# Holding the second layer's modulation sums on VectorE behind the feed-forward norm's inverse roots

## The chip, the core and the metric

The kernel runs on one core of a Trainium2 chip. The core has a matrix engine (TensorE, PE in the rows), two elementwise engines (VectorE, DVE; ScalarE, ACT), GpSimd (POOL) and SyncE (SP), which issues the transfers from HBM. Each engine takes its instructions in the order in which they stand in its own list, and starts one when the semaphores it waits for are there. The metric is the device time of one execution in microseconds (us).

## The reference

Two layers of a diffusion backbone over 256 latent and 256 context tokens of width 1024. What matters here is the conditioning of each layer and the feed-forward part of the first:

```python
def _rmsnorm(x, g):
    y = xf * lax.rsqrt(jnp.mean(xf * xf, axis=-1, keepdims=True) + EPS)
    return (y * g.astype(jnp.float32)).astype(x.dtype)
...
def _modulate(x, g, shift, scale):
    return _rmsnorm(x, g) * (1 + scale) + shift
...
def _adaln(cond, w_mod, b_mod):
    return jnp.split(jax.nn.silu(cond) @ w_mod + b_mod, N_MOD, axis=-1)
...
def _swiglu(x, w1, w3, w2):
    return (jax.nn.silu(x @ w1) * (x @ w3)) @ w2
...
# first layer, after its mixer
h = h + gt1 * o_lat
u_lat = _modulate(h, norm_ffn_g[layer], sh2, sc2)
g = g + cgt1 * o_ctx
tokens = jnp.concatenate([_modulate(g, norm_ffn_g[layer], csh2, csc2), u_lat], axis=1)
y = _swiglu(tokens, ffn_w1[j], ffn_w3[j], ffn_w2[j])
```

The second layer has its own `_adaln`: a product of a conditioning vector with a 1024 x 6144 matrix. It depends on nothing that the first layer computes.

## The kernel before, in words

The feature dimension lies on the 128 partitions, the 512 tokens along the free dimension: columns 0 to 255 are the context tokens (stream 0), 256 to 511 the latent ones (stream 1). `H` holds the residual, `Uhi` and `Ulo` the normed and modulated tokens, split in two parts, so that each matrix product is three matmuls (L162, L163, L164). The weights are loaded as `raw`, cast to `whi` on ScalarE and split off as `wlo` on VectorE (both L141); `whi` and `wlo` have six buffers each, `raw` four, which the modulation matrix shares. A scheduler at build time sets the order of every engine's list from the order of the code and from priorities; the order on the chip is then fixed.

The feed-forward norm of the first layer is `norm_T`, for stream 0 and then stream 1: squares on ScalarE (L318, L321), their sums on VectorE (L322, L324, tile `sqa`), a sum over the partitions on TensorE (L289, `ps_hg`), the inverse root on VectorE, and its spreading over the partitions on TensorE (L295), then per block of 128 features a product on VectorE (L336, `u`), the shift on ScalarE (L337, `Uhi`) and the remainder on VectorE (L338, `Ulo`). The inverse root (`rsqrt`, tile `rsq`) is eleven small VectorE operations, each on the result of the one before, L302, L303 and three rounds of

```python
        dve.tensor_tensor(b, y, y, op=OP.mult)
        dve.scalar_tensor_tensor(b, b, -0.5, v, op0=OP.mult, op1=OP.mult)
        latest_y[:] = [dve.scalar_tensor_tensor(y, b, 1.5, y, op0=OP.add, op1=OP.mult)]
```

which are L305, L306 and L307. Behind the norm stand the first four column tiles of the feed-forward layer (two of `w1`, two of `w3`). They are computed for stream 0 alone and then for stream 1 alone, 96 matmuls of 256 columns each; the tiles after them take all 512 columns at once. ScalarE takes the silu of the `w1` tiles (L756, `s`), VectorE multiplies it with the `w3` tiles (L759), and the result is split into `hh` (ScalarE) and `hl` (VectorE), both L167.

The second layer's modulation is worked out in the background by `mod1`, on VectorE: a block is 512 of the 6144 columns, and its sum over the 1024 rows is made of eight operations in each half, with two sums (`macc`, one for each conditioning vector) for blocks 0 to 3: L238 begins a sum, L240 adds to it (128 x 512). A half is 1 MB of `raw`, whose load is issued by SyncE (L113) in one list with the loads of the feed-forward weights (L116). When a block's sums are there, TensorE adds them over the partitions (L256) and the columns go to `modc` (L265). The generator is stepped between the tiles of the feed-forward layer. Block 0 lies in the last products of the mixer, block 1 in the feed-forward norm, blocks 2 to 7 in the feed-forward layer, 8 to 11 in the attention of the second layer. At the end stands the second layer's expert part, which streams its weights from HBM (`moe_u`, `moe_d`).

The prediction gives the line numbers of this kernel; those of the changed one are one or two higher from L237 on.

Of the kernel before, what the change touches and what calls it, by code (L numbers as in the profile page):

```python
# [15 lines left out]
OP = mybir.AluOpType  # L16
# [47 lines left out]
def body(tc, A, out):  # L64
    nc = tc.nc
    ctx = ExitStack()
    pe, act, dve, pool, sp = nc.tensor, nc.scalar, nc.vector, nc.gpsimd, nc.sync

    def sb(name, side="left"):
        return tc.tile_pool(name=name, bufs=1, side=side, reuse_waits="tile")  # L70
# [15 lines left out]
    def ps(tag, n=512):  # L86
        t = banks["pool"].tile([128, 512], F32, name="ps_" + tag, tag=tag, bufs=banks["bufs"][tag])
        return t[:, :n] if n != 512 else t
# [8 lines left out]
    def V(name, a=0, n=None):  # L97
        o, m = _VEC[name]
        return vec[:, o + a:o + a + (m if n is None else n)]
# [7 lines left out]
    def stream(src, kt=0, cols=0):  # L107

        turns.append(turns.pop(0))
        raw = turns[-1].tile([128, 2048], F32, name="raw", tag="raw", bufs=RING if len(turns) == 2 else None)  # L110
        if not kt:
            v = raw.rearrange("p (k c) -> p k c", k=4)
            sp.dma_start(v, src)  # L113
            return v
        v = raw[:, :kt * cols].rearrange("p (k c) -> p k c", k=kt)
        sp.dma_start(v, src.rearrange("(k p) c -> p k c", p=128))  # L116
        return v
# [28 lines left out]
    @contextmanager  # L146
    def behind(*ops):

        with ExitStack() as x:
            for op in ops or latest:  # L150
                x.enter_context(tc.issue_after(op.ins))
            yield
# [66 lines left out]
    def mod1(*groups):  # L219


        todo = [(g, blk, half) for g in groups for blk in g for half in range(2)]

        def load(i):
            g, blk, half = todo[i]
            return stream(A["w_mod"][1, blk, half])

        w, sums = load(0), []
        for i, (g, blk, half) in enumerate(todo):
            yield  # L230
            streams = range(2 if blk < 4 else 1)
            if half == 0:
                acc = [up.tile([128, 512], F32, name="macc", tag="macc", bufs=2) for _ in streams]
            for j in range(4):
                for s in streams:
                    c = csig[:, 4 * half + j, s:s + 1]
                    if half + j == 0:  # L237
                        dve.tensor_scalar(acc[s], w[:, j, :], c, None, op0=OP.mult)  # L238
                    else:
                        dve.scalar_tensor_tensor(acc[s], w[:, j, :], c, acc[s], op0=OP.mult, op1=OP.add)  # L240
            if i + 1 < len(todo):
                w = load(i + 1)
            if half == 0:
                continue
            sums += [(blk, s, a) for s, a in enumerate(acc)]
            if blk != g[-1]:
                continue
            p = ps("x")
            if blk in (4, 5, 8, 9, 10, 11):
                pe.matmul(p, ones1, acc[0], start=True, stop=True)  # L250
                r = {2: gt1r, 4: GF, 5: gt2r}[blk // 2][:, 512 * (blk % 2):512 * (blk % 2) + 512]
                dve.tensor_tensor(r, r, p, op=OP.add)
            else:
                n = 4 // len(sums)
                for q in range(4):
                    pe.matmul(p[32 * q:32 * q + 32, :], ones1[:, 0:32], sums[q // n][2], start=True, stop=True,  # L256
                              tile_position=(0, 32 * q))
                row = modp.tile([128, 512], F32, name="modrow", tag="modrow")
                act.copy(row, p)
                p = ps("x")  # L260
                for f in range(4):
                    pe.transpose(p[:, 128 * f:128 * f + 128], row[:, 128 * f:128 * f + 128], ident)
                v = p.rearrange("p (a g b) -> p g a b", a=4, g=4)
                for q, (b, st, _) in enumerate(sums):
                    dve.tensor_tensor(modc[1][:, 4 * b:4 * b + 4, st], v[:, n * q, :, 0], V("bm1", 4 * b, 4), op=OP.add)  # L265
            sums = []
# [40 lines left out]
            latest_y[:] = [dve.scalar_tensor_tensor(y, b, 1.5, y, op0=OP.add, op1=OP.mult)]  # L307
        return y

    latest_y = []  # L310

    def squares(tp, h, s, acc=None):

# [13 lines left out]
    def stream_rstd(tp, h, s):  # L327
        return rstd_rows(squares(tp, h, s), V("invd"), 2)

    def modulate(tp, h, rstd, s, ks, G, layer, which_shift, uhi, ulo, of=None):  # L330
        c = slice(256 * s, 256 * s + 256)
        of = of or c
        for k in ks:
            u = tp.tile([128, 2, NL], F32, name="u", tag="sq", bufs=3)[:, 0]
            shift = modc[layer][:, 8 * which_shift + k, 1 - s:2 - s]
            dve.scalar_tensor_tensor(u, h[:, k, of], G[:, k, 1 - s:2 - s], rstd, op0=OP.mult, op1=OP.mult)  # L336
            act.activation(uhi[:, k, c], u, AF.Identity, bias=shift)  # L337
            dve.scalar_tensor_tensor(ulo[:, k, c], u, shift, uhi[:, k, c].bitcast(F32), op0=OP.add, op1=OP.subtract)  # L338

    def norm_T(tp, *a):  # L340
        with tc.high_priority():
            for s in range(2):
                modulate(tp, a[0], stream_rstd(tp, a[0], s), s, range(KT), *a[1:])
# [7 lines left out]
    with sb("n0") as tp:  # L351
# [5 lines left out]
        acc = tp.tile([128, NTOK], F32, name="sqacc")  # L357
# [320 lines left out]
    acc = sop.tile([128, NTOK], F32, name="sqacc")  # L678
# [58 lines left out]

    finish()
    background.append(mod1((0,), (1,), (2,), (3,), (4,), (5,), (6, 7)))
    G2 = gain_cols("G2", 0, 4, "gf0")  # L740
    Uhi = up.tile([128, KT, NTOK], F32R, name="Uhi", tag="Uhi")
    Ulo = up.tile([128, KT, NTOK], F32R, name="Ulo", tag="Ulo")
    norm_T(nrm, H, G2, 0, 3, Uhi, Ulo)
    ffx = ExitStack()
    ffp = ffx.enter_context(sb("ffp", "right"))
    held = []
# [54 lines left out]
    Ulo = up.tile([128, KT, NTOK], F32R, name="Ulo", tag="Ulo")  # L801
    norm_T(nrm, H, G3, 1, 0, Uhi, Ulo)
    background.append(mod1((8,), (9,), (10,), (11,)))
    for _ in range(2):
        step()
# [94 lines left out]
    for g in range(2):  # L900
        c = slice(512 * g, 512 * g + 512)
# [109 lines left out]
    for g in range(2):  # L1011
# [3 lines left out]
        for t in range(2):  # L1015
# [7 lines left out]
            c = slice(512 * g, 512 * g + 512)  # L1023
# [315 lines left out]
    acc = [ps("mm") if i < 3 else ps("x") for i in range(4)]  # L1339
    for p, (t, g) in zip(acc, SETS):  # L1340
        scatter(p, DTS[1], t, g, 2, True, True)
    for p, (t, g) in zip(acc, SETS):
        c = slice(512 * g, 512 * g + 512)
# [144 lines left out]
```

## Time and profile before

| | |
|---|---|
| time, median of 3 runs | 1668.04 us (1666.72 to 1668.6) |
| the profiled execution | 1669.41 us, of which the trace spans 1667.6 us |
| TensorE busy | 1568.5 us, 94% of the span |
| VectorE busy | 721.0 us, 43% |
| ScalarE busy | 448.0 us, 27% |
| HBM read | 409.20 MB |

All times inside the program count from the start of the span. An engine's busy share is an average over stages with different limits: the feed-forward layer of the first layer lies at about 360 to 750 us, the expert part from about 960 us to the end, and each has to be read by itself. The granted clock of TensorE (PEclk) is a share of its full speed.

### The profile page before, as it was taken

To read this page: it belongs to the slowest core of one execution; us is meant where nothing else is said; L and a number is where in the kernel's file an instruction comes from. 1 tells how busy PE (TensorE), PEld (TensorE's weight loads), DVE (VectorE), ACT (ScalarE), POOL (GpSimd) and SP (SyncE) were. 2 spreads that over 40 slices of the span, in tenths; PEclk is the share of its full clock that TensorE was granted. 3 is DMA by queue.
4 is the path that set the end of the run, shared out by engine and by line. 5 is a ranking of instruction groups with operands and counts; after the bars stand their busy time and mean duration, and the time that the engine had idled before them with its cause. 6 is when DMAs were issued, how large, how long until landed. Compare 5 with 4: busy or idle time off the path is not lost. (4 is left out here: it accounts for less than half of the span.)

```text
span 1667.6 us, 25716 instructions
## 1 busy us (share of the span) xinstructions
PE 1568.5 (94%) x10916; PEld 943.6 (57%) x10916; DVE 721.0 (43%) x1367; ACT 448.0 (27%) x735; POOL 60.4 (4%) x58
## 2 busy tenths in 40 slices
PE   6998989999999999999999999999989999978896
PEld 3666767788778788898774644343334333311232
DVE  4787466586776434479628530020201131101132
ACT  3664334333222222234536420010101000100000
POOL 0023142000000000000000000000000000000000
PEclk9999999999999999999999989999999999999999
DMA  9411433833475233435432298979999999999996
GB/s 368 153 65 51 144 110 127 312 131 127 132 247 202 89 101 101 138 115 203 136 117 90 86 372 317 361 297 416 413 417 414 416 409 415 413 415 404 409 406 252
DMA packets 125669, 412.18 MB, mean 247 GB/s; under 512 B 9568, under 2 KB 52960, under 8 KB 101088
## 3 DMA queue, kind: packets, MB, share of 16 engines
q1 hardware_dynamic: 125536, 410.28, 64.4%
q8 instruction: 99, 1.62, 0.4%
q14 instruction: 34, 0.28, 0.0%
HBM read 409.20 MB, written 1.05 MB: 246 GB/s over the span
## 5 line engine op out<-in xcount | busy, mean ns | idle before, releaser
L1193 PE MATMUL ps_mm<-raw,X 128*32 128x512 f32 (+1 forms) x1920 | 217.2, 566 | 17.2 <-DMA raw<-in_moe_u 16.0
L162 PE MATMUL ps_mm<-Uhi,whi 128*128 128x512 f32 (+1 forms) x576 | 222.3, 392 | 5.8 <-ACT Uhi L337 3.4
L163 PE MATMUL ps_mm<-Ulo,whi 128*128 128x512 f32 (+1 forms) x576 | 223.7, 390 | 0.4 <-DVE Ulo L338 0.4
L164 PE MATMUL ps_mm<-Uhi,wlo 128*128 128x512 f32 (+1 forms) x576 | 223.3, 389 | 0.0
L141 ACT CAST whi<-raw 128x1024 fp32r<-128x1024 f32 x134 | 138.7, 1048 | 296.7 <-PE ps_mm L163 208.8
L141 DVE TENSOR_TENSOR wlo<-raw,whi 128x1024 fp32r<-128x1024 f32 x134 | 163.3, 1228 | 114.5 <-ACT whi L141 109.3
L1193 PEld LDWEIGHTS ps_mm<-raw,X 128*32 128x32 f32 x1920 | 66.7, 110 | 142.6 <-issue 96.2
L162 PEld LDWEIGHTS ps_mm<-Uhi,whi 128*128 128x128 f32 x576 | 109.0, 191 | 32.1 <-ACT Uhi L337 3.9
L1232 DVE COPY hT<-ps_x 128x384 f32<-128x384 f32 x24 | 13.4, 558 | 259.6 <-PE ps_x L1228 259.6
L163 PEld LDWEIGHTS ps_mm<-Ulo,whi 128*128 128x128 f32 x576 | 109.8, 191 | 24.3 <-issue 1.7
L164 PEld LDWEIGHTS ps_mm<-Uhi,wlo 128*128 128x128 f32 x576 | 110.0, 191 | 23.7 <-issue 1.7
L1252 PE MATMUL ps_py<-raw,hT 128*32 128x512 f32 x928 | 110.5, 602 | 13.3 <-DMA raw<-in_moe_d 12.4
L1232 ACT COPY hT<-ps_x 128x384 f32<-128x384 f32 (+1 forms) x24 | 10.2, 425 | 317.5 <-PE ps_x L1228 317.5
L240 DVE SCALAR_TENSOR_TENSOR macc<-raw,cond,macc 128x512 f32<-128x512 f32 x112 | 80.7, 748 | 5.5 <-DMA raw<-in_w_mod 4.8
L1211 DVE TENSOR_TENSOR hN<-hs,ps_mm 128x512 f32<-128x512 f32 (+1 forms) x24 | 15.4, 644 | 153.1 <-PE ps_mm L1193 135.5
L1252 PEld LDWEIGHTS ps_py<-raw,hT 128*32 128x32 f32 x928 | 31.1, 110 | 87.8 <-issue 66.9
L439 PE MATMUL ps_mm<-whi,Uhi 128*128 128x512 f32 x192 | 78.2, 407 | 0.0
L162 PE MATMUL ps_mm<-hh,whi 128*128 128x512 f32 (+1 forms) x224 | 77.7, 351 | 0.6 <-ACT hh L167 0.6
L163 PE MATMUL ps_mm<-hl,whi 128*128 128x512 f32 (+1 forms) x224 | 77.9, 349 | 0.0
L1193 PE MATMUL ps_mm<-wlo,X 128*32 128x512 f32 (+1 forms) x576 | 75.0, 554 | 2.4 <-DMA wlo<-in_moe_u 1.2
L164 PE MATMUL ps_mm<-hh,wlo 128*128 128x512 f32 (+1 forms) x224 | 77.2, 346 | 0.0
L441 PE MATMUL ps_mm<-whi,Ulo 128*128 128x512 f32 x192 | 77.2, 403 | 0.0
(304 smaller groups left out, 2252.8 us busy)
## 6 DMA issues: line engine op xcount, KB each, us to landing
raw<-in_moe_u SPq DMA_DIRECT2D x83, 1024.0 KB, 14.1
raw<-in_moe_d SPq DMA_DIRECT2D x58, 1024.0 KB, 14.8
raw<-in_w_mod SPq DMA_DIRECT2D x48, 1024.0 KB, 5.1
raw<-in_ffn_w SPq DMA_DIRECT2D x33, 1024.0 KB, 5.1
raw<-in_moe_u SPq DMA_DIRECT2D x37, 768.0 KB, 11.4
wlo<-in_moe_u SPq DMA_DIRECT2D x45, 512.0 KB, 11.4
whi<-in_moe_u SPq DMA_DIRECT2D x45, 512.0 KB, 11.4
whi<-in_moe_d SPq DMA_DIRECT2D x30, 512.0 KB, 11.4
```

What stands on the lines that cost most here:

```text
L141: latest[:] = act.copy(hi, v), dve.tensor_tensor(lo, v, hi.bitcast(F32), op=OP.subtract)
L162: pe.matmul(o, sh, mh, start=start, stop=False)
L163: pe.matmul(o, sh, ml, start=False, stop=False)
L164: return pe.matmul(o, sl, mh, start=False, stop=stop)
L240: dve.scalar_tensor_tensor(acc[s], w[:, j, :], c, acc[s], op0=OP.mult, op1=OP.add)
L439: pe.matmul(p, Uhi[:, u, tt], hi, start=u == 0, stop=False)
L441: pe.matmul(p, Ulo[:, u, tt], hi, start=False, stop=u == KT - 1)
L1193: m = pe.matmul(p[b][32 * q:32 * q + 32, :], X[e][:, k, 32 * g:32 * g + 32], w[2 * b + a], start=k == 0, stop=k == KT - 1, tile_position=( ...
L1211: dve.tensor_tensor(h[0][:, :fn], s[0][:, :fn], p[1], op=OP.mult)
L1232: (act.copy if c else dve.tensor_copy)(sub(hT_[:, 0, :], 2 * CAP * c, [(4 * CAP, n), (1, 2 * CAP)]), p.rearrange("p (c t) -> p c t", c=n))
L1252: pe.matmul(PY[e][0][32 * q:32 * q + 32, :], hT_[:, c, CAP * a + 32 * g:CAP * a + 32 * g + 32], w[a][:, 512 * col:512 * col + 512], start= ...
```

## The change

`norm_done` is filled, once the feed-forward norm's code has been recorded, with the last operation of the inverse root of stream 1 (the last L307). From then on each VectorE operation of `mod1` for a block other than 0 is recorded inside `behind(*norm_done)`, which puts it behind that operation in VectorE's list. No operation, transfer or buffer is added or taken away.

```diff
@@ -234,10 +234,11 @@
             for j in range(4):
                 for s in streams:
                     c = csig[:, 4 * half + j, s:s + 1]
-                    if half + j == 0:
-                        dve.tensor_scalar(acc[s], w[:, j, :], c, None, op0=OP.mult)
-                    else:
-                        dve.scalar_tensor_tensor(acc[s], w[:, j, :], c, acc[s], op0=OP.mult, op1=OP.add)
+                    with behind(*norm_done) if norm_done and blk else ExitStack():
+                        if half + j == 0:
+                            dve.tensor_scalar(acc[s], w[:, j, :], c, None, op0=OP.mult)
+                        else:
+                            dve.scalar_tensor_tensor(acc[s], w[:, j, :], c, acc[s], op0=OP.mult, op1=OP.add)
             if i + 1 < len(todo):
                 w = load(i + 1)
             if half == 0:
@@ -307,7 +308,7 @@
             latest_y[:] = [dve.scalar_tensor_tensor(y, b, 1.5, y, op0=OP.add, op1=OP.mult)]
         return y
 
-    latest_y = []
+    latest_y, norm_done = [], []
 
     def squares(tp, h, s, acc=None):
 
@@ -741,6 +742,7 @@
     Uhi = up.tile([128, KT, NTOK], F32R, name="Uhi", tag="Uhi")
     Ulo = up.tile([128, KT, NTOK], F32R, name="Ulo", tag="Ulo")
     norm_T(nrm, H, G2, 0, 3, Uhi, Ulo)
+    norm_done[:] = latest_y
     ffx = ExitStack()
     ffp = ffx.enter_context(sb("ffp", "right"))
     held = []
```

The lists of SyncE and GpSimd stay as they were, row for row. Those of the other three differ in one place only, from the norm of stream 1 to the first full tiles of the feed-forward layer. VectorE's list before, at the end of the inverse root of stream 1 (`rsq_2573`):

```order
L307 SCALAR_TENSOR_TENSOR rsq_2573<-rsq_2574,rsq_2573 128x2
L240 SCALAR_TENSOR_TENSOR macc<-raw,cond,macc 128x512
L305 TENSOR_TENSOR rsq_2574<-rsq_2573 128x2
L240 SCALAR_TENSOR_TENSOR macc<-raw,cond,macc 128x512
L306 SCALAR_TENSOR_TENSOR rsq_2574<-rsq_2574,rsq_2572 128x2
L240 SCALAR_TENSOR_TENSOR macc<-raw,cond,macc 128x512
L307 SCALAR_TENSOR_TENSOR rsq_2573<-rsq_2574,rsq_2573 128x2
L240 SCALAR_TENSOR_TENSOR macc<-raw,cond,macc 128x512 x2
L336 SCALAR_TENSOR_TENSOR u<-H,G_2489,ps_hg 128x256 x3
```

The same place in the changed kernel:

```order
L308 SCALAR_TENSOR_TENSOR rsq_2573<-rsq_2574,rsq_2573 128x2
L167 TENSOR_TENSOR hl<-s_2662,hh 128x256
L306 TENSOR_TENSOR rsq_2574<-rsq_2573 128x2
L307 SCALAR_TENSOR_TENSOR rsq_2574<-rsq_2574,rsq_2572 128x2
L308 SCALAR_TENSOR_TENSOR rsq_2573<-rsq_2574,rsq_2573 128x2
L239 TENSOR_SCALAR macc<-raw,cond 128x512 x2
L337 SCALAR_TENSOR_TENSOR u<-H,G_2489,ps_hg 128x256 x3
```

The additions of block 1 are gone from between the steps of the root. Over the whole root (L302 to the last L307) six L240 have left, and one L240 and two L238 from ahead of it; of the two L759 and two L167 that stood between its steps the second pair has moved to the end of the norm (L759 ahead of its last two L338, L167 behind them).

Where block 1 went: VectorE's list in the changed kernel behind the last product of the norm, where `wlo` are the splits of weights for later tiles.

```order
L167 TENSOR_TENSOR hl<-s_2688,hh 128x256
L241 SCALAR_TENSOR_TENSOR macc<-raw,cond,macc 128x512 x2
L141 TENSOR_TENSOR wlo<-raw,whi 128x1024
L241 SCALAR_TENSOR_TENSOR macc<-raw,cond,macc 128x512
L141 TENSOR_TENSOR wlo<-raw,whi 128x1024
L761 TENSOR_TENSOR s_2662<-s_2662,ps_mm 128x256
L141 TENSOR_TENSOR wlo<-raw,whi 128x1024
L167 TENSOR_TENSOR hl<-s_2662,hh 128x256
L761 TENSOR_TENSOR s_2688<-s_2688,ps_mm 128x256
L241 SCALAR_TENSOR_TENSOR macc<-raw,cond,macc 128x512
L141 TENSOR_TENSOR wlo<-raw,whi 128x1024
```

Directly behind these rows stand nine more L241 in one run, then the fifth `wlo`, the last L241 of block 1 and the sixth `wlo`. Before, five of block 1's L240 stood behind the last L336, the last of them ahead of the fourth `wlo`.

TensorE's list before, where the root of stream 1 is spread over the partitions (`ps_hg_2586`; `ps_mm_2636`, `_2637`, `_2752` and `_2753` are the four tiles):

```order
L163 MATMUL ps_mm_2753<-Ulo_2492,whi_2748 128x256
L164 MATMUL ps_mm_2753<-Uhi_2491,wlo_2749 128x256
L295 MATMUL ps_hg_2586<-ident_69,rsq1_2573 128x128 [waits DVE_49]
L295 MATMUL ps_hg_2586<-ident_69,rsq1_2573 128x128
L162 MATMUL ps_mm_2636<-Uhi_2491,whi_2628 128x256 [waits Activation_49]
L162 MATMUL ps_mm_2637<-Uhi_2491,whi_2632 128x256
```

And in the changed kernel:

```order
L163 MATMUL ps_mm_2753<-Ulo_2492,whi_2748 128x256
L296 MATMUL ps_hg_2586<-ident_69,rsq1_2573 128x128 [waits DVE_49]
L296 MATMUL ps_hg_2586<-ident_69,rsq1_2573 128x128
L164 MATMUL ps_mm_2753<-Uhi_2491,wlo_2749 128x256
L162 MATMUL ps_mm_2753<-Uhi_2491,whi_2748 128x256
L163 MATMUL ps_mm_2753<-Ulo_2492,whi_2748 128x256
L164 MATMUL ps_mm_2753<-Uhi_2491,wlo_2749 128x256
```

The spreading stood behind all 96 matmuls of stream 0; now the last seven of them stand behind it. In the same way L289 for stream 1 has moved ahead of five matmuls of the third tile, `ps_mm_2752`.

## Rows read from the trace of the kernel before

**Rows 1.** The page, part 1: busy time, share of the span, instructions
```profile
PE 1568.5 (94%) x10916; PEld 943.6 (57%) x10916; DVE 721.0 (43%) x1367; ACT 448.0 (27%) x735; POOL 60.4 (4%) x58
```

**Rows 2.** Timeline of TensorE: start, duration, instruction, idle time before it and releaser
```profile
358.01 0.71 PE L295 MATMUL ps_hg<-ident,rsq 128*128 128x128 f32 x4
...
360.41 0.66 PE L262 MATMUL ps_x<-ident,modrow 128*128 128x128 f32 x4 [0.70 <-ACT modrow L259]
360.82 0.73 PE L162 MATMUL ps_mm<-Uhi,whi 128*128 128x256 f32 x4
...
369.63 0.50 PE L289 MATMUL ps_hg<-vec,sqa 128*128 128x1 f32 x4
369.99 0.37 PE L163 MATMUL ps_mm<-Ulo,whi 128*128 128x256 f32 x1
...
372.72 0.28 PE L164 MATMUL ps_mm<-Uhi,wlo 128*128 128x256 f32 x1
...
376.92 1.22 PE L295 MATMUL ps_hg<-ident,rsq 128*128 128x128 f32 x4 [3.92 <-DVE rsq L307]
379.25 1.22 PE L162 MATMUL ps_mm<-Uhi,whi 128*128 128x256 f32 x4 [1.11 <-ACT Uhi L337]
...
392.29 0.39 PE L162 MATMUL ps_mm<-Uhi,whi 128*128 128x512 f32 x1
...
425.92 1.07 PE L256 MATMUL ps_x<-macc,ones 128*32 128x512 f32 x8
```

**Rows 3.** Stretches: length, busy time of each engine, granted clock, DMA share, GB/s
```profile
374.00:376.00 2.00, 0.00 (x0) 0.00 (x0) 2.00 (x8) 0.00 (x0) 0.00 (x0) 0.98 0.00 0
376.00:378.00 2.00, 1.08 (x4) 0.93 (x4) 2.00 (x6) 0.00 (x0) 0.00 (x0) 0.50 0.47 78
...
383.00:384.00 1.00, 1.00 (x11) 1.00 (x10) 1.00 (x3) 0.58 (x2) 0.00 (x0) 1.00 0.00 0
```

**Rows 4.** Timeline of VectorE
```profile
355.06 0.16 DVE L307 SCALAR_TENSOR_TENSOR rsq<-rsq,rsq 128x2 f32<-128x2 f32 x1
355.26 0.16 DVE L305 TENSOR_TENSOR rsq<-rsq 128x2 f32<-128x2 f32 x1
...
368.67 0.42 DVE L324 TENSOR_TENSOR sqa<-sqa 128x256 f32<-128x256 f32 x1
369.01 0.75 DVE L240 SCALAR_TENSOR_TENSOR macc<-raw,cond,macc 128x512 f32<-128x512 f32 x1
370.17 0.16 DVE L302 TENSOR_SCALAR rsq<-ps_hg 128x2 f32<-128x2 f32 x1 [0.41 <-PE ps_hg L289]
370.25 0.41 DVE L759 TENSOR_TENSOR s<-s,ps_mm 128x256 f32<-128x256 f32 x1
...
373.03 0.42 DVE L759 TENSOR_TENSOR s<-s,ps_mm 128x256 f32<-128x256 f32 x1 [0.43 <-PE ps_mm L164]
...
376.70 0.16 DVE L307 SCALAR_TENSOR_TENSOR rsq<-rsq,rsq 128x2 f32<-128x2 f32 x1
...
378.18 1.26 DVE L336 SCALAR_TENSOR_TENSOR u<-H,G,ps_hg 128x256 f32<-128x256 f32 x3
...
398.91 1.23 DVE L141 TENSOR_TENSOR wlo<-raw,whi 128x1024 fp32r<-128x1024 f32 x1 [3.58 <-ACT whi L141]
```

**Rows 5.** Waits of TensorE from 390 to 860 us: total, times, longest
```profile
PE ps_mm L162 <- ACT hh L167: 0.6, 1, 0.6
```

**Rows 6.** Timeline of SyncE: issue of a feed-forward load
```profile
391.09 0.37 SPq L116 DMA_DIRECT2D raw<-in_ffn_w  x1
```

**Rows 7.** Timeline of ScalarE: the cast of that load
```profile
397.83 1.05 ACT L141 CAST whi<-raw 128x1024 fp32r<-128x1024 f32 x1 [4.10 <-PE ps_mm L163]
```

**Rows 8.** Stretches, as in rows 3, late in the program
```profile
900.00:950.00 50.00, 48.18 (x278) 29.12 (x277) 34.77 (x87) 29.95 (x70) 0.00 (x0) 1.00 0.11 32
...
1400.00:1500.00 100.00, 87.54 (x850) 28.05 (x841) 14.04 (x26) 11.41 (x30) 0.00 (x0) 1.00 1.02 415
```

**Rows 9.** Waits of the transfer queue from 840 to 1000 us, the longest
```profile
SPq L131 <- PE ps_mm L1022: 38.6, 4, 30.0
```

## The prediction, made before the changed kernel ran

> **What bounds the kernel now.** I read the busy shares first: TensorE works for 94% of the span [rows 1], so time is to be won only where it stands still or runs slowly. The list of its waits, then its timeline, show one large hole ahead of the expert part. TensorE ends the 96 stream-0 products of the first feed-forward tiles at about 373.0, and then does nothing for 3.92 us, until the inverse root of stream 1 is there (L295 at 376.92, released by VectorE's last L307); it waits another 1.11 us for the first `Uhi` of stream 1 and begins that stream at 379.25 [rows 2]. The stretches show what that costs besides: TensorE is idle and VectorE fully busy from 374 to 376, and from 376 on the granted clock is 0.50, the 1.2 of its two levels of 1.2 and 2.4 GHz; only at 383 is it 1.00 throughout [rows 3]. VectorE's timeline says why the root is late. Its eleven dependent steps need 0.19 us each where nothing stands between (355.06 to 355.26), some 2.1 us in all; for stream 1 they run from 370.17 to 376.86, that is 6.7 us [rows 4], since VectorE's list has six 0.75 us additions of block 1, two L759 and two L167 between them. So the stall belongs to VectorE's order.
>
> After it TensorE is covered: from 390 to 860 us it waits once, for 0.6 us [rows 5]. What is won at 379 should therefore still be there at 860.
>
> **The change, part by part.**
>
> *Ahead of the root.* Two L238 and an L240 leave the place ahead of L302. That alone gives little: the squares' sum would end near 368.4 instead of 369.09 (368.67 and 0.42) [rows 4], but L289 also waits for its turn on TensorE, and there it moves up by five products. Stream 0 takes 96 products in 12.02 us (360.82 to 372.72, and 0.12 for the last), of which L289 takes 0.36 (369.63 to 369.99); so one product takes 11.66 / 96 = 0.12 us [rows 2]. L289 then goes at 369.63 - 0.60 = 369.03, and L302, 0.54 behind it as now (370.17 - 369.63), at 369.57.
>
> *Inside the root.* Ten steps of 0.19, one of 0.16, and the L759 and L167 that stay, 0.33 each (0.41 less the overlap of about 0.08, by which L302 and L759 lie 0.08 apart for a 0.16 operation [rows 4]): 2.06 + 0.66 = 2.72. The last L307 ends at 369.57 + 2.72 = 372.29, instead of 376.86. The second L759, which waited 0.43 us for a product of TensorE in the middle of the root (373.03 [rows 4]), is out of it. The first one needs the third tile, whose last product TensorE now leaves at 369.99 instead of 369.63, with some 0.2 more until it is written, 370.2; it is due at 369.57 + 4 x 0.19 = 370.33, so it just does not wait. If it does, by at most the 0.43 of its neighbour, the sum shrinks by that.
>
> *The spreading and the first product.* TensorE reaches L295 with seven stream-0 products still to do, at 372.84 - 7 x 0.12 = 372.0. It waits until 372.29 and 0.06 more (376.86 to 376.92), 372.35, and then needs the 0.71 us that L295 took for stream 0 at full clock (358.01 [rows 2]) rather than 1.22. The spread root is there at 373.06. VectorE has two L238 to do meanwhile, 0.88 us from 372.25, so L336 starts at about 373.1; the list of before put the first stream-1 product 1.07 us behind L336 (378.18 to 379.25 [rows 2, 4]), which gives 374.2. The seven products left over cover TensorE until about 373.9. Term one: 379.25 - 374.2 = 5.1 us.
>
> *The clock.* Stream 1 took 13.04 us (379.25 to 392.29), stream 0 11.66 without its L289 [rows 2]: term two is 1.4 us, if the clock stays up. The remaining holes are of about 0.3 us each (372.0 to 372.35, 373.9 to 374.2). The nearest rows on either side: a hole of 0.70 us at 360.41 was followed by products 0.12 us apart, one of 3.92 by the clock of 0.50 [rows 2, 3]; 0.3 lies with the first. Bounds: 0 and 1.4; I take 1.4. On this the Trainium skill ("TensorE: Matmul & The Clock Gate", Part 1) adds that the number of products that run at the low level differs between runs of one kernel; by that the term would be other than 1.4 in the runs timed, in either direction, and nothing here can tell, since one execution is all there is.
>
> *Where the sixteen operations go.* Two L238 lie under L295, as said, and cost nothing. On ScalarE one cast (L167) moves behind the eight shifts of stream 1, and the L167 of VectorE that needs it has moved with it. The fourteen L240 go behind the norm, around and behind the first four weight splits. Two things wait for them. Block 1's sums are due on TensorE at 425.92, and the first product on the weights of the fifth split directly behind, at 426.9 [rows 2]; both 6.5 us earlier now, 419.4 and 420.4. I bound their lateness from above: were the load of those weights issued no earlier than before, at 391.09 [rows 6], it would be there at 397.83, when its cast waited for TensorE and no longer for the load; cast 1.05 [rows 7], split 1.23, and the run of nine L240 at 0.75 ahead of the split, 6.75 [rows 4]: 397.83 + 1.05 + 1.23 + 6.75 = 406.9. That leaves 12.5 us to block 1's due time. VectorE has room there: ahead of the fifth split alone it idled 3.58 us (398.91 [rows 4]). Cost 0; without the cover each operation would cost its 0.75.
>
> *Later.* The lists do not differ anywhere else, so everything behind moves up with TensorE.
>
> *Sum.* 5.1 + 1.4 = 6.5 us. The profiled execution took 1669.41 (span 1667.6 and 1.8 around it) and becomes 1662.9. It was 1.37 us above the median of the runs, 1668.04; for these I forecast 1668.04 - 6.5 = 1661.5 us, 0.39% faster. A difference under 0.2% (3.3 us) is about what a measurement of this kernel cannot tell from none. Own bounds of the sum: 5.1 - 0.43 = 4.7 if the clock term is lost and the first L759 waits, and some 7.3 if TensorE reaches the last steps with no hole at all (0.5) and L302 comes 0.3 earlier.
>
> **The rivals.**
>
> *The expert part swallows it.* From 1400 to 1500 us TensorE is busy 87.5 of 100 us while the transfers are at 1.02 of their engines' time and move 415 GB/s [rows 8]: this part is bound by its weights. If their stream began at a time that the feed-forward layer does not set, the end would stay where it is: 1668.0. Against it: from 900 to 950 the transfers are busy for 0.11, and the issuing queue waits 38.6 us for TensorE's second-layer output products (L1022), 30.0 at a stretch [rows 8, 9]; so the stream is released by TensorE and moves up with it. The Trainium skill ("Perfetto Trace Analysis", Roofline) puts a single core's ceiling at its 16 DMA engines, about 435 GB/s. By that ceiling a part that runs at 415 has nothing from an earlier TensorE, and the sum is 0; the trace agrees about the rate, not about the start. I give 8 in 100 that half or more of the gain goes this way (1664.8 to 1668).
>
> *The clock falls all the same*, because of the two small holes: only term one is kept, 1662.9. 8 in 100.
>
> *The deferred additions hold up the weights* (slower). VectorE works in order: at 373.03 a waiting L759 held the root's ready next step back [rows 4]. In the new list the fifth split waits behind nine L240 and behind its load, which SyncE issues in its own order behind a modulation load that itself needs a buffer freed by block 1. With no spare time at all TensorE would wait for the 6.75 of additions, a load (6.7, from 391.09 to 397.83) and a cast, 1.05: 14.5 us, against 6.5 won; 1668.04 + 8.0 = 1676.0. It decides only once the split is late by more than the 12.5 us of spare time above. 3 in 100.
>
> *The hole is not closed*, since something else is late at once (the squares of ScalarE, the buffer of `ps_hg`): then a few tenths are won, 1667.5. The rows speak against it: TensorE's wait ends with L307, and L307 is behind additions that are ready long before. 2 in 100.
>
> **How the numbers follow.** My forecast has 79 in 100, the clock's fall 8, the swallowed gain 8, no closing 2, slower 3. The predicted time is the first, 1661.5. Its own range is 1660.2 (1668.04 - 7.3, less 0.5 for the spread of a median of runs that lie 1.9 apart) to 1663.8 (1668.04 - 4.7 and 0.5), and that contains the clock's fall. It holds 87 in 100 if the working is right; I widen the upper side by 0.7, to 1664.5, for part of the swallowed gain: 1660.2 to 1664.5. Faster by over 0.2% means below 1664.7: the first two cases and a little of the third, 0.88. Within 0.2%: 0.09. Slower: 0.03.
>
> **What would show it.** In the changed kernel's trace TensorE's wait for the root of stream 1 is below 0.5 us instead of 3.92, and L295 takes about 0.7; L302 to the last L307 take about 2.7 us; the first stream-1 product is at about 374.2 and the first 512-column product at about 385.8; the granted clock stays at 1.00 from 370 to 390; TensorE still waits under 1 us from 385 to 855, and the expert part is shifted as a whole by 6.5. I would be wrong if the clock is at 0.50 anywhere there, if a wait for `wlo` or `macc` appears between 400 and 440, or if the waits for `raw` in the expert part grow by the gain.

## The result, and the profile after

The changed kernel takes 1660.01 us (median of 5 runs, 1657.64 to 1661.21), the kernel before 1668.6 beside it (5 runs): a ratio of 0.9945 [0.9933, 0.9956] (in brackets, here and below, the 95% interval), 8.6 us faster. The forecast of 1661.5 is 1.5 us too high, and the measured time lies 0.2 us below the low end of the range, 1660.2. The stall and the clock came out as forecast; the size of the whole did not, and the runs further down say how much of that is the kernel and how much the scatter of executions. One execution further down, of the version with the pair held, took 1965.47 us at a granted clock of 0.75 and is left out of that version's median and ratio.

The profiled execution took 1661.21 us, its span 1659.4. The page of the changed kernel, part 1, answers to [rows 1]:

```profile
PE 1564.2 (94%) x10916; PEld 941.5 (57%) x10916; DVE 721.8 (43%) x1367; ACT 448.1 (27%) x735; POOL 60.4 (4%) x58
```

TensorE is busy for 4.3 us less with the same 10916 instructions; the mean granted clock of this execution is 0.988, that of the one before 0.985. Its timeline in the changed kernel, which answers to [rows 2] (line numbers are one higher here):

```profile
359.85 0.74 PE L162 MATMUL ps_mm<-Uhi,whi 128*128 128x256 f32 x4
...
368.07 0.50 PE L290 MATMUL ps_hg<-vec,sqa 128*128 128x1 f32 x4
...
370.92 0.28 PE L163 MATMUL ps_mm<-Ulo,whi 128*128 128x256 f32 x1
371.32 0.71 PE L296 MATMUL ps_hg<-ident,rsq 128*128 128x128 f32 x4
...
372.58 0.28 PE L164 MATMUL ps_mm<-Uhi,wlo 128*128 128x256 f32 x1
373.14 0.61 PE L162 MATMUL ps_mm<-Uhi,whi 128*128 128x256 f32 x3 [0.28 <-ACT Uhi L338]
...
384.92 0.39 PE L162 MATMUL ps_mm<-Uhi,whi 128*128 128x512 f32 x1
...
418.63 1.06 PE L257 MATMUL ps_x<-macc,ones 128*32 128x512 f32 x8
```

Stream 0 begins 0.97 us earlier than in the trace of before; ahead of it the programs are the same, so the place has to be read from its own start. From the first product of stream 0 to the first 512-column product it took 392.29 - 360.82 = 31.47 us [rows 2], and takes 384.92 - 359.85 = 25.07: 6.40 us less, where the sum said 6.5. Of these, 18.43 - 13.29 = 5.14 lie ahead of the first stream-1 product (term one said 5.1), and 13.04 - 11.78 = 1.26 behind it (term two said 1.4). The 5.14 are three pieces of [rows 2, 4] and the rows here: the square sum comes 0.59 us earlier after the start of stream 0, the root takes 4.04 less, and from the spread to the first product it takes 1.82 instead of 2.33, since the spread runs at the upper clock. The spread of the root (L296) stands in the middle of the stream-0 products now, and the 3.92 us hole is gone.

VectorE's timeline in the changed kernel, to [rows 4]:

```profile
368.61 0.16 DVE L303 TENSOR_SCALAR rsq<-ps_hg 128x2 f32<-128x2 f32 x1 [0.97 <-PE ps_hg L290]
368.80 0.17 DVE L304 TENSOR_SCALAR rsq<-rsq 128x2 int32<-128x2 int32 x1
...
369.39 0.42 DVE L761 TENSOR_TENSOR s<-s,ps_mm 128x256 f32<-128x256 f32 x1
...
370.30 0.16 DVE L308 SCALAR_TENSOR_TENSOR rsq<-rsq,rsq 128x2 f32<-128x2 f32 x1
370.38 0.42 DVE L167 TENSOR_TENSOR hl<-s,hh 128x256 fp32r<-128x256 f32 x1
370.72 0.15 DVE L306 TENSOR_TENSOR rsq<-rsq 128x2 f32<-128x2 f32 x1
...
371.10 0.16 DVE L308 SCALAR_TENSOR_TENSOR rsq<-rsq,rsq 128x2 f32<-128x2 f32 x1
371.18 0.88 DVE L239 TENSOR_SCALAR macc<-raw,cond 128x512 f32<-128x512 f32 x2
...
387.94 6.05 DVE L241 SCALAR_TENSOR_TENSOR macc<-raw,cond,macc 128x512 f32<-128x512 f32 x9
393.91 1.22 DVE L141 TENSOR_TENSOR wlo<-raw,whi 128x1024 fp32r<-128x1024 f32 x1
```

The root runs from 368.61 to 371.26, 2.65 us instead of 6.7. The first held operation stands directly behind it, and the run of nine additions is over at 393.99, some 25 us before the sums of block 1 go to TensorE (418.63). Stretches of the changed kernel, in the columns of [rows 3], show the granted clock at its upper level where it had been at 0.50:

```profile
360.00:392.00 32.00, 31.58 (x232) 29.59 (x232) 30.29 (x71) 15.38 (x31) 0.00 (x0) 1.00 0.28 97
...
372.00:374.00 2.00, 1.70 (x12) 1.29 (x11) 1.99 (x6) 1.31 (x3) 0.00 (x0) 1.00 0.00 0
374.00:376.00 2.00, 2.00 (x18) 2.00 (x18) 2.00 (x6) 1.06 (x3) 0.00 (x0) 1.00 0.03 8
376.00:378.00 2.00, 2.00 (x19) 2.00 (x18) 2.00 (x7) 0.95 (x3) 0.00 (x0) 1.00 0.00 0
```

Behind the place nothing gives it back. TensorE's only wait from 385 to 860 us in the changed kernel, to [rows 5]:

```profile
PE ps_mm L162 <- ACT hh L167: 0.3, 1, 0.3
```

From the page of the changed kernel, part 5, its products on the experts' weights; the last number is the wait for weights:

```profile
L1195 PE MATMUL ps_mm<-raw,X 128*32 128x512 f32 (+1 forms) x1920 | 216.8, 565 | 18.2 <-DMA raw<-in_moe_u 16.8
```

The kernel before waited 16.0 us there; a swallowed gain would have made it some 22 (16.0 and 6.5, an estimate).

### The profile page after: what moved, and what is told of

It reads as the page before. It is cut to its first block, busy times and chain, and to the rows that moved or that the text cites. A ratio compares the mean times of both kernels' runs of the same rounds, so it can differ in the third digit from the quotient of the medians.

```text
span 1659.4 us, 25717 instructions
## 1 busy us (share of the span) xinstructions
PE 1564.2 (94%) x10916; PEld 941.5 (57%) x10916; DVE 721.8 (43%) x1367; ACT 448.1 (27%) x735; POOL 60.4 (4%) x58
## 5 line engine op out<-in xcount | busy, mean ns | idle before, releaser
L1254 PE MATMUL ps_py<-raw,hT 128*32 128x512 f32 x928 | 108.8, 594 | 13.7 <-DMA raw<-in_moe_d 12.9
L1234 ACT COPY hT<-ps_x 128x384 f32<-128x384 f32 (+1 forms) x24 | 10.2, 425 | 317.9 <-PE ps_x L1230 317.9
L241 DVE SCALAR_TENSOR_TENSOR macc<-raw,cond,macc 128x512 f32<-128x512 f32 x112 | 80.2, 747 | 5.3 <-DMA raw<-in_w_mod 4.6
```

The lines of the kernel that those rows point to most:

```text
L1234: (act.copy if c else dve.tensor_copy)(sub(hT_[:, 0, :], 2 * CAP * c, [(4 * CAP, n), (1, 2 * CAP)]), p.rearrange("p (c t) -> p c t", c=n))
L1254: pe.matmul(PY[e][0][32 * q:32 * q + 32, :], hT_[:, c, CAP * a + 32 * g:CAP * a + 32 * g + 32], w[a][:, 512 * col:512 * col + 512], start= ...
```

## The experiments

For each kernel I give the *place*: from the first product of stream 0 to the first 512-column product in its trace. It is 31.47 us in the first trace of before and 25.07 in that of the changed kernel. Some kernels do extra work; none leaves out part of the computation. Theory A: the change acts at this place alone, and what exceeds 6.4 is the scatter of executions. Theory B: it acts elsewhere too, and is worth 8.5.

**Both kernels again.** No edit.

> The kernel of before, unchanged, timed against itself. Theory A (the change acts at one place, the norm of stream 1, and is worth 6.4 us there; the other 2 us between the medians, 8.6, are spread between executions): the two sets of runs of one program differ by up to 1 to 2 us in their medians, and a second profile of it starts its first matmul anywhere between 10.9 and 11.6 us, so that the 0.97 us by which the changed kernel was already ahead at 366 us appears or not by chance. Theory B (the change is worth some 8.5 us and acts elsewhere too): ratio within 0.999 to 1.001, the first matmul again at about 11.57 and stream 1 of the norm again at about 379.25.

> The changed kernel once more. Theory A: from the last stream-0 products to the first 512-column product it gains 6.4 us again (within 0.1), the lead ahead of that place lies anywhere between -0.5 and 1.1 us, and the median of the runs is 5 to 9 us under before, whichever way the spread falls. Theory B: the lead ahead of the place is again 0.9 to 1.1, the lead grows again by 0.25 at about 490 us and by 0.35 between 660 and 720 us, and the median is 8 to 9 us under before.

Measured: before 1668.31 (ratio to the runs of before beside it 0.9994 [0.9984, 1.0004]), place 31.52; changed 1661.34, 0.9953 [0.9941, 0.9966], place 25.06. Stream 0 begins at 362.36 in this trace of before and at 360.82 in the first one: the same program drifts by 1.5 us ahead of the place. The place itself repeats to 0.05 in these two traces of each kernel.

**The hole filled, the root left late.** Thirty products into a spare bank behind the last stream-0 product of the kernel before (`last` is that product; `fill` is 30 where the two `w3` tiles are computed):

```diff
...
+                if fill and m == 0 and s == 0:
+                    with behind(last):
+                        idle = ps("md")
+                        for j in range(fill):
+                            pe.matmul(idle[:, :NL], w2[0][0][:, j % KT, :], Uhi[:, j % KT, t], start=True, stop=True)
...
```

> The kernel of before with 30 more matmuls of 256 columns on TensorE (into a bank that nothing reads) behind the last stream-0 product, 3.6 us of work in the hole of 3.92 us; VectorE's order is as before. It takes the clock alone. My terms: the spreading of the root takes 0.71 instead of 1.22 us, stream 1 takes 11.66 instead of 13.04 us, so 1.9 us less in all, with the root as late as before (TensorE's L295 still at about 376.9 plus the lead of this execution). Rival (the slow products are due to late Uhi and Ulo, not to the clock): stream 1 still takes about 13 us and nothing is gained.

TensorE's timeline there:

```profile
362.04 0.74 PE L162 MATMUL ps_mm<-Uhi,whi 128*128 128x256 f32 x4
...
374.06 3.76 PE L430 MATMUL ps_md<-Uhi,whi 128*128 128x256 f32 x30
378.15 0.71 PE L295 MATMUL ps_hg<-ident,rsq 128*128 128x128 f32 x4 [0.33 <-DVE rsq L307]
379.98 0.73 PE L162 MATMUL ps_mm<-Uhi,whi 128*128 128x256 f32 x4 [1.11 <-ACT Uhi L337]
...
391.63 0.40 PE L162 MATMUL ps_mm<-Uhi,whi 128*128 128x512 f32 x1
```

The root is exactly as late as before (L295 16.11 us behind the start of stream 0; 16.10 in [rows 2]), yet the spread takes 0.71 instead of 1.22, and stream 1 takes 11.65 instead of 13.04. The place is 29.59, 1.88 us shorter. This is the clock's share alone: the hole cost its own length and 1.9 us of low clock behind it. The wait of 1.11 us that is left did not bring the clock down. The other reading, that late `Uhi` and `Ulo` make stream 1 slow, falls: the first `Uhi` comes as long behind the spread as before (the wait is 1.11 us again), and stream 1 is fast. The whole took 1664.32, 0.9975 [0.9966, 0.9984]: some 4 us less and not 1.9, and the one trace lacks a later low-clock stretch too (below).

**Six more operations between the rounds.** The kernel before with six VectorE operations of 128x512 added among the root's steps, two to a round (`more` is a tile of ones; `stuff` names it twice while the norm of stream 1 is recorded):

```diff
...
+            for o in stuff:
+                with behind(m):
+                    m = dve.scalar_tensor_tensor(o, o, 0.5, o, op0=OP.mult, op1=OP.add)
...
```

> The kernel of before with six more VectorE operations of 128x512 on a tile that nothing else reads, two in each round of the inverse root of stream 1; TensorE's list is as before. My theory (each operation between the steps of the root delays stream 1 by its whole duration): the root's end moves by 6 x 0.67 to 6 x 0.75 = 4.0 to 4.5 us, TensorE's hole grows from 3.9 to about 8.2 us, and the program takes 4.0 to 4.5 us longer, 0.24% to 0.27%. Rival (the hole is set by something that VectorE's order does not reach): under 0.5 us.

TensorE's timeline there:

```profile
381.53 1.22 PE L295 MATMUL ps_hg<-ident,rsq 128*128 128x128 f32 x4 [7.06 <-DVE rsq L311]
383.87 1.22 PE L162 MATMUL ps_mm<-Uhi,whi 128*128 128x256 f32 x4 [1.12 <-ACT Uhi L341]
...
398.05 0.40 PE L162 MATMUL ps_mm<-Uhi,whi 128*128 128x512 f32 x1
```

The idle time ahead of L295 grew from 3.92 to 7.06 us, by 3.14 for six operations. That is less than the 4.0 to 4.5 expected: each takes 0.69 us, of which 0.60 pass before the next operation starts, 3.6 in all, and some 0.4 of it falls into the time in which the second L759 had waited for its product (0.43 [rows 4]; here it does not wait). Apart from that, what stands between the rounds is paid for by TensorE. The place is 35.76, 4.29 us longer; that this lies in the range set for the root is luck, since 1.14 of it is stream 1, which takes 14.18 instead of 13.04 at the lower clock. The whole took 1671.88, 1.0021 [1.0011, 1.003]. (The whole grew by less than the place; this trace lacks the later stretch as well.)

**The first three operations free again.** The changed kernel, with two L239 and one L241 not held:

```diff
-                    with behind(*norm_done) if norm_done and blk else ExitStack():
+                    with behind(*norm_done) if norm_done and (blk, half, 2 * j + s) > (1, 0, 2) else ExitStack():
```

> The changed kernel, except that the first three modulation additions on VectorE (three of 128x512, 0.41 us each) are free again to run before the last round of the second stream's root. They are the ones that stood ahead of that root's last steps in the kernel before; the others stay held. If each operation that stands in or ahead of the chain delays it by its own length, the spread of the inverse root comes about 0.5 to 1.3 us later than in the changed kernel (371.3), and the gain at the place is 5.1 to 5.9 instead of 6.4. If only what stands between the rounds counts, the gain stays 6.4. Theory C and theories A and B say the same of this kernel as of the changed one in all other places.

TensorE's timeline there:

```profile
362.29 0.74 PE L162 MATMUL ps_mm<-Uhi,whi 128*128 128x256 f32 x4
...
374.31 0.64 PE L296 MATMUL ps_hg<-ident,rsq 128*128 128x128 f32 x4
376.06 0.62 PE L162 MATMUL ps_mm<-Uhi,whi 128*128 128x256 f32 x3 [1.11 <-ACT Uhi L338]
...
387.84 0.39 PE L162 MATMUL ps_mm<-Uhi,whi 128*128 128x512 f32 x1
```

The place is 25.55, a gain of 5.92, the upper edge of what the first reading gave. The spread stands 12.02 us behind the start of stream 0 (11.47 in the changed kernel), now behind all stream-0 products, so that TensorE waits 1.11 us for `Uhi` with nothing to do. The clock stays at 1.00 in every 2 us stretch up to 388. So holding the three ahead of the root is worth 0.5 of the 6.4 us; the other 5.9 come from the rest: the six inside the root, the pair that moved with them, and the clock. The whole: 1662.57, 0.9959 [0.9945, 0.9972].

**The start of attention covered, in both kernels.** At about 880 us TensorE stands still for 0.61 and 0.59 us, and in the first traces of both kernels its granted clock then fell. Timeline of TensorE in the kernel before:

```profile
879.04 1.12 PE L889 MATMUL ps_mm<-kT,QT 64*128 64x512 f32 x2 [0.61 <-ACT e L895]
880.75 0.85 PE L931 MATMUL ps_hg<-ident,e 128*128 128x128 f32 x4 [0.59 <-DVE e L897]
```

The stretch behind it, in the columns of [rows 3]:

```profile
882.00:884.00 2.00, 2.00 (x4) 0.50 (x4) 2.00 (x7) 0.91 (x3) 0.00 (x0) 0.50 0.91 365
```

That is worth 2.85 us (by the time to a later product of the same attention, against traces without the stretch), and no such stretch was in the traces of the two kernels with filled hole and with six more operations. Theory C was that the 2 us beyond 6.4 are this stretch, which would fall less often in the changed kernel. Ten transposes were meant to cover the two waits (`cover` is called behind the first four transposes of `e` and behind the first product of the scores that follow):

```diff
...
+    def cover(last):
+        with behind(last):
+            idle = ps("md")
+            for j in range(5):
+                pe.transpose(idle[:, :128], ident, ident)
...
```

> The kernel before, with ten 128x128 transposes of the identity into a spare PSUM bank at the start of attention, five behind the first four transposes of e and five behind the first product of the scores that follow, where TensorE stood idle for 0.61 and 0.59 us and its granted clock then fell to 0.50 for 6.8 us. Nothing of the computation is left out; the list of the attention's instructions behind that place comes out in another order than before. Theory C (the 2 us beyond the place are the low-clock stretch at the start of attention, worth 2.85 us, that falls in some executions and not in others, and in fewer of the changed kernel's): clock 1.00 from 870 to 890, and 1.5 to 2.5 us faster than before, 1666 to 1667. If the stretch does not matter for the difference: the same gain here as in the changed kernel with the same cover.

> The changed kernel with the same ten transposes at the start of attention. Theory C: 6.4 us below the covered kernel before, some 0.5 to 1.5 us below the changed kernel, 1659 to 1660. Theory B (the change acts systematically elsewhere as well, ahead of the place or behind it): 8 to 8.5 us below the covered kernel before. Theory A with chance alone (the other 2 us are the scatter of few executions): 6.4 below the covered one, and the changed kernel run again beside it is 6.5 to 7 below before.

> The changed kernel unchanged, for more executions. Chance alone: 6.4 to 7 us below the kernel before in this call. A systematic part beyond the place: 8 to 8.5 below, again. In its trace: the gain at the place 6.4 once more; the start of the first stream's products ahead of the place, where both programs are the same, anywhere between 359.8 and 362.4 if it is chance, and between 359.8 and 360.3 as in the two profiles of the changed kernel so far if it is not.

Before, covered: 1667.44, 0.9995 [0.9986, 1.0004]; changed, covered: 1659.13, 0.9947 [0.9933, 0.996]; changed, uncovered: 1659.7, 0.995 [0.9936, 0.9963]. The clock stays at 1.00 at the start of attention in both covered traces, as expected. But only the first wait is gone; the second is left, with five transposes behind it. In the covered kernel before:

```profile
881.87 0.66 PE L939 MATMUL ps_hg<-ident,e 128*128 128x128 f32 x4 [0.58 <-DVE e L905]
```

And the covered kernel before is 0.8 us faster by its ratio, with an interval that holds zero, not the 1.5 to 2.5 that theory C gave. The difference of the covered pair is still 8.3 us, and that of the uncovered kernel 8.5: by the numbers set beforehand both speak for theory B. Theory C falls, by a count too: over all traces without the cover the stretch is in four of five of before and in five of seven of the changed kernel, with the same two waits (0.61 to 0.62 and 0.58 to 0.59) in every one of them. At 2.85 us each that is a difference of 0.2. One of the traces of the changed kernel without it (the first of the last four below):

```profile
875.00:877.00 2.00, 2.00 (x12) 1.17 (x11) 2.00 (x8) 1.75 (x6) 0.00 (x0) 1.00 0.94 374
```

Stream 0 of the uncovered one begins at 361.81, inside the span of before: the part ahead of the place is chance. But the trace of the covered kernel before has a place of 32.59, 1.12 longer than the first, with the granted clock at 0.50 for 10.2 us instead of 6.8, while the changed one has 25.05 again. Theory D: the kernel before pays another price at the place in another execution.

**Three more profiles of before, and the last two operations held.** The second edit, on the covered changed kernel, holds behind the root the L761 that still stood in it (and with it the L167 that needs its result):

```diff
...
+            with behind(*norm_done) if f0 + i + t.start == 0 else ExitStack():
-            dve.tensor_tensor(S[i][:, t], S[i][:, t], p[:, t], op=OP.mult)
+                dve.tensor_tensor(S[i][:, t], S[i][:, t], p[:, t], op=OP.mult)
...
```

> The kernel before unchanged, for a further profile of it. The mean gain over all executions so far is 8.1 us, with the attention's low-clock stretch covered in both it is 8.2, and five profiles of kernels with the change show 5.9 to 6.4 at the place against the first profile of before. Theory D: the low-clock stretch at the place (6.8 us in the first profile of before and in the second, 10.2 us in that of the covered kernel before, where the place cost 1.12 more) is a different length in different executions, and longer on average than in the one that the prediction was read from; then of these three profiles at least one shows 10.2 us and 1.1 us more at the place, and the mean over all six is 0.4 to 1.1. Theory E: it is 6.8 us in all of them and the place costs the same, so that what is beyond 6.4 lies in no place that the profiles have shown.

> As the run ahead of it: the kernel before, one more profile. Theory D: 6.8 or 10.2 us of granted clock 0.50 at the place, and with 10.2 us the first stream's products end 1.1 us later. Theory E: 6.8 us.

> As the two runs ahead of it: the kernel before, one more profile. Theory D: 6.8 or 10.2 us of granted clock 0.50 at the place, and with 10.2 us the first stream's products end 1.1 us later. Theory E: 6.8 us.

> The changed kernel with the cover at the start of attention, and with the last two operations that still stood between the rounds of the second stream's root (one product with the silu part and one low part, 128x256, 0.42 us each) held behind the root too. By the row of the changed kernel each delays the next step of the root by about 0.3 us, so the root is spread 0.6 us earlier (370.7 when the products of the first stream start at 359.9), the last idle pieces of TensorE there (0.40 and 0.28 us) go, and the gain at the place is 6.9 instead of 6.4. Over the whole, 0.5 us is less than the executions scatter: 1658.6 against the 1659.1 of the covered kernel. If ScalarE or the PSUM bank is held up by the late operation instead: no gain, or up to 1 us lost.

The three places of before are 32.68, 31.50 and 31.20. Timeline of TensorE in the first of them:

```profile
359.63 0.73 PE L162 MATMUL ps_mm<-Uhi,whi 128*128 128x256 f32 x4
...
375.68 1.22 PE L295 MATMUL ps_hg<-ident,rsq 128*128 128x128 f32 x4 [3.92 <-DVE rsq L307]
378.02 1.22 PE L162 MATMUL ps_mm<-Uhi,whi 128*128 128x256 f32 x4 [1.11 <-ACT Uhi L337]
...
392.31 0.40 PE L162 MATMUL ps_mm<-Uhi,whi 128*128 128x512 f32 x1
```

Its stretches:

```profile
374.00:376.00 2.00, 0.32 (x1) 0.32 (x2) 2.00 (x7) 0.00 (x0) 0.00 (x0) 0.50 0.23 33
...
382.00:384.00 2.00, 2.00 (x12) 2.00 (x11) 2.00 (x6) 0.91 (x2) 0.00 (x0) 0.50 0.00 0
384.00:386.00 2.00, 2.00 (x18) 2.00 (x18) 1.98 (x3) 0.00 (x0) 0.00 (x0) 0.97 0.00 0
```

Both waits are those of [rows 2] to the hundredth; stream 1 takes 14.29 us instead of 13.04. The clock was down already while TensorE stood still, and stayed down until 384. Theory D holds: over the six traces of before (one of them with attention covered) the place is 31.47, 31.52, 32.59, 32.68, 31.50 and 31.20, in the mean 31.83. That is 0.36 more than in the first, just under the 0.4 to 1.1 that theory D gave. In eight traces of the changed kernel, those below and the covered one included, it is 25.05 to 25.19, in the mean 25.09. The gain at the place is 6.7 us.

The version with the pair held has a place of 24.53, a gain of 6.94 (expected: 6.9); its timeline:

```profile
360.34 0.73 PE L162 MATMUL ps_mm<-Uhi,whi 128*128 128x256 f32 x4
...
371.27 0.71 PE L296 MATMUL ps_hg<-ident,rsq 128*128 128x128 f32 x4
...
373.02 0.28 PE L164 MATMUL ps_mm<-Uhi,wlo 128*128 128x256 f32 x1
373.13 0.59 PE L162 MATMUL ps_mm<-Uhi,whi 128*128 128x256 f32 x3
```

Stream 1 follows stream 0 without a wait. It took 1657.7, 0.9941 [0.9926, 0.9957], the fastest version here, though its distance to the covered one is within their uncertainty.

**The changed kernel, four times more.** No edit.

> The changed kernel unchanged. Chance (nothing beyond the place): with these the mean over all its executions comes up to 1661 to 1661.8, 6.5 to 7.3 below before, and the low-clock stretch at about 961 is 13.7 us in two or more of these four profiles. A part beyond the place: the mean stays at 1660.0 to 1660.6, 7.7 to 8.4 below before; if it is the stretch at 961, it is 10.2 us in at least three of the four.

> As the run ahead of it. The gain at the place is 6.4 again; 961 shows 10.2 or 13.7 us of granted clock 0.50.

> As the two runs ahead of it. The gain at the place is 6.4 again; 961 shows 10.2 or 13.7 us of granted clock 0.50.

> As the three runs ahead of it. The gain at the place is 6.4 again; 961 shows 10.2 or 13.7 us of granted clock 0.50.

Ratios 0.9957, 0.9965, 0.9956 and 0.996, with intervals from 0.9942 to 0.9978. The places: 25.19, 25.07, 25.17, 25.05. These 25 executions average 1661.0, 6.8 below the 12 of before beside them; so the 8.5 of the third profile of the changed kernel did not hold. All runs together: 87 of before, mean 1668.28, scattered by 1.8; 41 of the changed kernel, mean 1660.75, scattered by 1.9. The gain is 7.5 us, with 0.7 of uncertainty (95%: 1.96 times the root of 1.8²/87 + 1.9²/41). By the four groups that were timed side by side it is 9.2, 7.7, 7.7 and 6.8. The 7.5 lies between the two expectations and settles neither.

The four traces differ from most of before in one stretch, at the start of the expert part. The first trace of the changed kernel has its granted clock at 0.50 there for 10.2 us:

```profile
961.80:972.00 10.20, 9.58 (x133) 6.85 (x134) 4.07 (x23) 4.89 (x12) 0.00 (x0) 0.50 1.01 424
972.00:975.40 3.40, 3.40 (x40) 1.05 (x36) 0.00 (x0) 0.00 (x0) 0.00 (x0) 1.00 0.98 380
```

So has the first trace of before:

```profile
969.80:980.00 10.20, 9.58 (x130) 6.68 (x134) 3.96 (x23) 4.88 (x12) 0.00 (x0) 0.50 1.02 426
```

The trace of before with the place of 32.68 goes on at 0.50 for 3.4 us more:

```profile
964.40:974.60 10.20, 9.59 (x136) 8.43 (x138) 4.95 (x33) 2.51 (x6) 0.00 (x0) 0.50 1.01 424
974.60:978.00 3.40, 3.40 (x39) 1.47 (x33) 0.97 (x2) 2.97 (x8) 0.00 (x0) 0.50 1.01 420
```

The stretch is 13.7 us long in four of the six traces of before, and in one of the ten of kernels that hold the operations; from the first product of attention to the first of the experts' second weights the longer one costs 1.1 to 1.4 us. If that is no accident, it is worth, as an estimate, (4/6 - 1/10) x 1.2 = 0.7, and 6.7 + 0.7 is close to the 7.5 measured. The 10.2 us in all four of the last traces is what a part beyond the place was expected to show. Against it, the kernels with the filled hole and with six more operations hold none of the sixteen and show 10.2 as well: with them it is four of eight, and 0.5. No run was made that takes this stretch away, so it stays open.

Whether anything beyond the place is real stays open too. The spans of the five traces of before and the seven of the changed kernel without the cover differ by 7.5 us in the mean: 6.6 at the place, 0.2 ahead of it, where the programs are the same, and 0.7 behind it, with an uncertainty of 0.9. The gain at the place, 6.7 over all traces, is itself uncertain by 0.5, since the six places of before scatter by 0.6; so it agrees with 7.5 and its 0.7.

## Why the prediction came out as it did

*What bounds the kernel: right.* What is taken out of the root's steps comes back, and what is put in is paid for, except where VectorE would have waited anyway (0.4 of 3.6 us with six more operations).

*Ahead of the root: right.* With the 0.97 us by which stream 0 begins earlier, the square sum was forecast for 369.03 - 0.97 = 368.06 and came at 368.07, the root's first step for 368.60 and came at 368.61.

*Inside the root: right.* 2.72 forecast, 2.65 measured. L761 did not wait, as forecast; L167 cost 0.23, not 0.33 (from 370.30 to 370.72, 0.42 instead of 0.19).

*The spreading and the first product: right.* TensorE waited 0.28 for the spread (forecast 0.35), reckoned as in the forecast from the start of the last product, 370.92, and 0.12; the spread took 0.71; the first stream-1 product was forecast for 373.23 and came at 373.14.

*The clock: right in kind, its price read from one execution.* It stays up from 360 to 392 in the changed kernel. Term two, 1.4, measures 1.26 against the trace that it was read from. But that trace is one execution of a price that varies: stream 1 takes 13.04 in four of six traces of before, within 0.3, and about 14.3 in two. Against their mean the term is 1.6. In single traces the term is anything from 1.0 to 2.5 (stream 1 at 12.76 to 14.29). The prediction named this itself, that one execution is all there is, and still gave the term the upper bound 1.4, which is its own value in that execution. The passage that it cited there, the Trainium skill ("TensorE: Matmul & The Clock Gate", Part 1), says that the number of products at the low level differs between runs of one kernel. The six traces agree: the longest place of before is 1.5 us above the shortest.

*Where the sixteen operations go: right.* Nothing waits for them; TensorE's one wait of 0.3 us behind the place is for another tile, and was there before, with 0.6 [rows 5].

*Later, and the rivals: right.* The gain reaches the end; the expert part does not swallow it, the additions hold up no weights, and the clock does not fall at the place in any of the nine traces with all sixteen held, nor in the one with thirteen.

*The sum: the step that failed.* 6.5 at the place was right to 0.1 for the trace it was read from, and 6.7 is the mean over six. What failed is the step from it to a range. Its low end, 1660.2, was 1668.04 less 7.3, a sum in which term two could not be above 1.4, less 0.5 for the spread of a median, taken from three runs that lay 1.9 apart. 87 runs of before reach from 1663.8 to 1671.7, and 41 of the changed kernel from 1657.3 to 1663.8. With a scatter of 1.8 to 1.9, the median of five moves by about 1 us, and the difference of two such medians by about 1.4 (an estimate). The 8.6 first measured is a draw from that around 7.5 or somewhat less; the range left no room for it below 1660.2. The mean of the 41, 1660.75, lies in the range, and of five executions drawn from them the median is under 1660.2 in about one of three draws (an estimate from these 41): that the first five fell outside, by 0.2 us, is in good part chance. Up to 0.8 us of the mean gain itself (7.5 against 6.7) is not accounted for.

## What to carry to other kernels

Where a chain of short dependent operations shares an in-order engine with long independent ones, hold the long ones until the chain is done, and count first what covers them afterwards: here nine of sixteen operations, with a pair that moved with them, cost 5.1 us in and ahead of the chain, the slower spread included, and the sixteen cost nothing behind it. A hole on TensorE has two prices, its length and the slow products behind it; the second is read from several traces, since one execution shows only one of its values. Before giving a range, look how far single executions of the same program lie apart, and add that to the bounds of the sum.

## What the runs showed of the hardware

A hole of 3.92 us on TensorE cost 1.9 us of low clock besides its length (the filled hole against the first trace), and up to 1.2 more in other executions of the same program with the same hole. Waits of 1.11 us alone left the granted clock at 1.00 in two kernels (the filled hole and the three operations free); two waits of 0.6 us at the start of attention were followed by 0.50 in four of five traces of the kernel before and in five of seven of the changed one, and by 1.00 in the others, with the same instructions around them. So whether the clock falls is not decided by the length of the wait alone.
